# Token products with the weights' low parts last, and another order of normed rows at two stage boundaries, in a hybrid decoder layer

## Chip, cores and metric

The kernel runs on 1 core of one Trainium2 chip. The metric is the time of one execution in microseconds of the device. Engines are named as in the profile: PE is TensorE (matrix products), PEld its weight loads, ACT is ScalarE, DVE is VectorE, POOL is GpSimd, SP is SyncE, which issues the loads.

## The reference

One layer on a sequence of 256 tokens with 1024 channels, all in float32, conditioned by a vector `c`:

```python
c_act = silu(c);  mod = c_act @ w_ada + b_ada;  sh1, sc1, g1, sh2, sc2, g2, sh3, sc3, g3 = split(mod, 9)
u = modulate(rmsnorm(h, norm_ff1), sh1, sc1)
h = h + 0.5 * g1 * swiglu(u, w_ff1_gate, w_ff1_up, w_ff1_down)      # 2816 hidden columns
u = modulate(rmsnorm(h, norm_mix), sh2, sc2)
h = h + g2 * token_mixing(u, ...)     # proj = u @ w_in; gated linear attention and block attention, 4 heads each
u = modulate(rmsnorm(h, norm_ff2), sh3, sc3)
h = h + 0.5 * g3 * swiglu(u, w_ff2_gate, w_ff2_up, w_ff2_down)
return rmsnorm(h, norm_final)
```

`rmsnorm(x, g)` is `x * rsqrt(mean(x*x) + 1e-6) * g`, `modulate(x, sh, sc)` is `x * (1 + sc) + sh`, and `swiglu` is `(silu(x @ w_gate) * (x @ w_up)) @ w_down`.

## The kernel before

Activations lie with channels on the 128 partitions: 8 blocks of channels by 256 tokens. Each product of full precision is made of three products of rounded parts: with `x = xh + xl` and `w = wh + wl`, it is `wh*xh + wh*xl + wl*xh`, and all three are added up in one accumulation bank (`mm3`). A weight tile of 128 by about 1024 is loaded by SP (`load`, 8 buffers called `raw`); ACT rounds it to its high part (`hi`), DVE takes the difference to get the low part (`lo`); both have 6 buffers (`split`). `Stream` holds the tiles in the order of their use: `more` or `prepare` does load, `hi` and `lo` of the next tile, `high` does load and `hi` and returns a function that issues the `lo` later, `take` hands out the oldest prepared tile, and `ahead(n)` prepares until n are ready. Instructions of PE, ACT and DVE stay in the order in which the program issues them (`InOrder`), so an instruction that waits holds all those behind it on its engine.

Between two parts of the layer stands a `Boundary`. It ends the last accumulations (`finish`), adds them to `h` block by block and makes rounded rows of `h` without the norm. `first` runs the first 24 blocks of products (8 channel blocks by 3 weight tiles, `mm3` each) with these unnormed rows, so that PE works while the mean square is made. On the way, at block 14, PE sums the squares and POOL takes the power -0.5 (line 388); later `spread` (line 426) brings 1/rms to all partitions by two transposes on PE. Then `modulate` makes the normed rows by a written-out order: step `n` k (DVE) multiplies row block k by the gain and 1/rms, `h` k (ACT) adds the shift and rounds it to the high part, `l` k (DVE) makes the low part. In the same order `A` prepares a whole weight tile, `H` loads one and makes its high part, `L` makes the low part of the oldest tile that `H` began, `b` (ACT) copies 1/rms out of its bank (`rbs`), and `s` loads a table for ACT. `MOD1` is the order of the first boundary, `MOD2` that of the second. The block order is `IN_TURN` = 0 4 1 5 2 6 3 7 for accumulations; `MOD1` goes by 0 to 7.

Behind the first boundary the next products are those of `gv_t`, a `Tokens` (line 780): here the rows are the stationary operand and the weight tile is the moving one, 4 weight tiles of 2 channel blocks each, 2 halves of the tokens (`t`), 2 halves of 264 columns: 96 products. The inner loop takes, for one bank at a time,

```python
mm(to, b, u2[0][:, k, blk(t)], wh[:, ws])
mm(to, b, u2[1][:, k, blk(t)], wh[:, ws])
mm(to, b, u2[0][:, k, blk(t)], wl[:, ws], stop=(k == KD - 1))
```

Then the three banks of `first` are multiplied by `rbs` (`normed`: `col` on ACT, `sg` on DVE, `gqk` on ACT), the banks of `gv_t` are copied (`glt`, then `v`), and the order `MIX` runs the mixing: jobs of column products (`F`, 48 or 24 products) between the steps of the two attentions. Its first words are `F lowrank F logits`: the logits need `glr`, which ACT copies behind the tiles that the first `F` prepares. A second `Tokens`, `mv_t`, has one piece of 512 columns.

Behind the second boundary `START2` (line 58) gives the order: `t` runs two gate products together (`both_gates`: at each channel block the two banks take turns), `i` scales the three banks of `first`, `A` prepares a tile, `o` runs `low_last` (16 products with the high part of a tile, then 8 with the low part), `s` and `m` make the first hidden rows, `r` splits them in parts, and `g` goes on with a third row. Then come a gate-and-up job of 48 products and the first down job, for which five tiles are prepared.

Of the kernel before, what the change touches and what calls it, by code (L numbers as in the profile page):

```python
# [20 lines left out]
KD = D // P  # L21
# [31 lines left out]
         q7 l4 a6 a7 l5"""  # L53
LAST = """n0 q0 n1 q1 a0 s0 n2 q2 a1 s1 n3 q3 a2 s2 n4 q4 a3 s3 n5 q5 a4 s4 n6 q6 a5 s5 n7 q7 z7 s6 a6 a7"""
LATE = "l6 l7"
MOD1 = "A H n0 h0 n1 h1 l0 n2 h2 l1 n3 h3 l2 l3 L n4 h4 n5 h5 l4 n6 l5 A h6 n7 h7 l6 l7 A b"
MOD2 = "A H s n0 h0 n4 h4 n1 l0 h1 l4 n5 h5 l1 n2 h2 l5 n6 h6 l2 n3 h3 l6 n7 h7 l3 l7 L A b"
START2 = "t i0 i1 i2 A o s0 s2 m0 g m1 g r0 r1 g"
GV = 528
EPS = 1e-6  # L60
NEG = -1e30
# [28 lines left out]
def hybrid_layer(ctx: ExitStack, tc: tile.TileContext, x, xT, cols, tri_d, mask_d, rel_bias,  # L90
# [16 lines left out]
    class InOrder:  # L107


        def __init__(self, engine):  # L110
            self.engine, self.last, self.on = engine, None, False
# [19 lines left out]
    def name(s):  # L131
        n_made[0] += 1
        return f"{s}_{n_made[0]}"

    def bank():
        return pp.tile([P, 512], F32, tag="b", name=name("b"), bufs=8)
# [4 lines left out]
    def big():  # L141
        return wk.tile([P, KD, S], F32, tag="b8", name=name("b8"), bufs=2)
# [6 lines left out]
    def mid(shape, dt=F32):  # L149
        return wk.tile(shape, dt, tag="s4", name=name("s4"), bufs=MID)  # L150

    def row(shape=(P, S), dt=F32, tag="r1", bufs=6):
        return wk.tile(list(shape), dt, tag=tag, name=name(tag), bufs=bufs)

    def blk(i):
        return slice(i * P, (i + 1) * P)

    def wblk(i):
        return slice(i * P + i // 4 * 32, (i + 1) * P + i // 4 * 32)

    def play(order, ops):

        for word in order.split():
            op = word.rstrip("0123456789")
            ops[op](*[int(x) for x in word[len(op):]])
# [42 lines left out]
    def mm(out_ap, bank_t, lhsT, rhs, stop=False):  # L208

        first = id(bank_t) not in opened  # L210
        i = ten.matmul(out_ap, lhsT, rhs, start=first, stop=stop, skip_group_check=True)
        last_mm[0] = i
        if first:
            opened[id(bank_t)] = (i, bank_t)
        else:
            tc.add_manual_dep(i.ins, opened[id(bank_t)][0].ins.name, DEP, reason="the bank's first matmul")
        return i

    def mm3(out_ap, bank_t, w, wsl, a, stop=False):

        wh, wl = w
        ah, al = a
        mm(out_ap, bank_t, wh[:, wsl], ah)
        mm(out_ap, bank_t, wh[:, wsl], al)
        mm(out_ap, bank_t, wl[:, wsl], ah, stop=stop)
# [36 lines left out]
    stream = Stream()  # L262

    class Pipe:
# [10 lines left out]
        def run(self, job):  # L275
            due = job()
            self.fetch()
            self.due = due
            stream.ahead(self.depth)

        def next(self):
            if self.todo:
                self.run(self.todo.pop(0))
# [182 lines left out]
    def low_last(b, base, w, u):  # L466

        for part in range(2):
            for k in IN_TURN:
                for r in range(2 - part):  # L470
                    mm(b[:, base:base + S], b, w[part][:, wblk(k)], u[r][:, k, :S], stop=(k == KD - 1 and part == 1))
# [42 lines left out]
    class Boundary:  # L514
# [46 lines left out]
        def first(self, parts, late, sum_at=14):  # L561


            blocks = [(k, b, w) for k in IN_TURN for b, w in parts]
            for at, (k, b, w) in enumerate(blocks):
                if at == sum_at:
                    self.rms.sums()
                    self.steps(late)
                if at == sum_at + 2 * len(parts):
                    self.rms.spread()  # L570
                mm3(b[:, :SW], b, w, wblk(k), (self.uh[:, k, :SW], self.ul[:, k, :SW]), stop=(k == KD - 1))

# [36 lines left out]
    ada_raw, lead_raw, ws, us = {}, {}, {}, {}  # L609
# [39 lines left out]
    rests = {}  # L649
# [24 lines left out]
    for f in range(LEAD, NF):  # L674
        stream.unit(("gu1", f), gu1[f - LEAD])
        work1.append(("f", f))
        n = sum(1 for x, _ in work1 if x == "d")
# [22 lines left out]
    for f in range(NF):  # L700
        stream.unit(("gu2", f), gu2[f])
        work2.append(("f", f))
        n = sum(1 for x, _ in work2 if x == "d")
# [33 lines left out]
    hid = Hidden()  # L737
    steps = [hid.add(b) for b in lead_banks]
# [13 lines left out]
    def mix_constants():  # L752
        ctri = [load(tri_d[:, i]) for i in range(3)]
        for to, src in ((mask, mask_d), (rel, rel_bias), (wlr_s, wlr)):
            nc.sync.dma_start(to, src)
        for i in range(3):
            act.activation(tri[:, i], ctri[i][:, :512], AF.Copy)
        bank()

        nc.gpsimd.memset(rrow, NEG)  # L760
        for bucket, first, last in BUCKETS:
            nc.gpsimd.tensor_copy(rrow[:, 127 + first:128 + last],
                                  rel[:, bucket:bucket + 1].to_broadcast([4, last - first + 1]))
        nc.gpsimd.dma_start(rdram, rrow)
        nc.gpsimd.dma_start(bias, bass.AP(tensor=rdram.tensor, offset=rdram[:, :].offset,
                                          ap=[[1, P], [NREL, 4], [1, S]]))
        vec.memset(glr, 1.0)
# [12 lines left out]
    class Tokens:  # L780


        def __init__(self, *widths):
            self.width, self.pieces = sum(widths), []
            for n in widths:
                at = self.pieces[-1].stop if self.pieces else 0
                self.pieces.append(slice(at, at + n))

        def run(self, i):
            if i == 0:  # L790
                self.banks = [[bank() for _ in self.pieces] for _ in range(2)]
            wh, wl = stream.take()
            for kk in range(2):
                k = 2 * i + kk
                for t in range(2):
                    for b, piece in zip(self.banks[t], self.pieces):
                        ws = slice(kk * self.width + piece.start, kk * self.width + piece.stop)
                        to = b[:, :piece.stop - piece.start]
                        mm(to, b, u2[0][:, k, blk(t)], wh[:, ws])
                        mm(to, b, u2[1][:, k, blk(t)], wh[:, ws])  # L800
                        mm(to, b, u2[0][:, k, blk(t)], wl[:, ws], stop=(k == KD - 1))

    def columns(done):

# [17 lines left out]
    pipe.depth = AHEAD2  # L822
    h = bd.new
    fb = [bank() for _ in range(3)]
    gv_t = Tokens(GV // 2, GV // 2)
    bd.first([(b, stream.take()) for b in fb], LATE)
    u2 = bd.modulate(MOD1)
    gk, gq = [row(tag="gqk", bufs=4) for _ in range(2)], [row(tag="gqk", bufs=4) for _ in range(2)]
    mk, mq = mid([P, 4, S]), mid([P, 4, S])
    mv_t = Tokens(512)  # L830
    got = {}

    def to_sbuf(dst, scale=1.0):
# [36 lines left out]
    for i, (to, scale) in enumerate(((gk[0], 1.0), (gk[1], 1.0), (gq[0], GLA_SCALE))):  # L870
        t, col = bd.normed(fb[i], scale)
# [59 lines left out]
    at = [mid([P, 4, S]), mid([P, 4, P])]  # L931
# [217 lines left out]
    pipe.depth = AHEAD4  # L1149
    hid = Hidden()  # L1150
    sb = [bank(), bank()]
    sg, m, steps = {}, {}, hid.add(sb[1], 2)

    def both_gates():
        together([(b, 0, stream.take()) for b in sb], u3)
# [7 lines left out]
    def first_product(i):  # L1163
# [3 lines left out]
        else:  # L1167
            vec.tensor_tensor(out=m[1], in0=sg[2], in1=sb[0][:, :S], op=ALU.mult)

    play(START2, {"A": stream.more, "t": both_gates, "i": normed_part, "s": first_silu, "m": first_product,  # L1170
                  "r": lambda i: hid.add_rows(m[i], i), "o": lambda: low_last(sb[1], S, stream.take(), u3),
                  "g": lambda: next(steps)})
    dbanks = []
    for at, (what, n) in enumerate(work2[3:-1]):
        pipe.run(gate_up(hid, u3) if what == "f" else down(n, dbanks, hid))
# [23 lines left out]
    o = big().rearrange("p k s -> p (k s)")  # L1199
    rs = bd.rms.rs  # L1200

    def scaled(engine, t, at, n):

        src, dst = turned_o[t][at // 512][:, at % 512:at % 512 + n], o[:, t * D + at:t * D + at + n]
        if engine is act:
            act.activation(dst, src, AF.Copy, scale=rs[:, t:t + 1])
        else:
            vec.tensor_scalar(dst, src, rs[:, t:t + 1], None, op0=ALU.mult)
        return out[blk(t), at:at + n], dst

    pieces = [scaled(vec, 0, 512, 256), scaled(act, 0, 0, 512), scaled(vec, 0, 768, 256), scaled(vec, 1, 512, 512)]
# [102 lines left out]
```

## Time and profile before

| | us |
|---|---|
| median of 3 runs | 571.19 |
| lowest and highest run | 570.15, 572.04 |
| the profiled execution | 570.41 |
| its span in the trace | 568.6 |

The profile is that of one execution. Its span runs from the first to the last recorded instruction; the time of the execution is 1.8 us longer. In lists of instructions each row has the start in us from the span's start, the length, the engine, line 115 (where a helper records every operation), the operation, output and inputs by the program's names, their form, and a count where several in a row are merged. A bracket at the end names how long the engine stood before and what ended that. Rows of PE overlap, since products are pipelined: their starts tell the pace.

### The profile page before, as it was taken

What the parts mean: (1) busy time and instruction counts of PE and PEld (TensorE: products, weight loads), DVE (VectorE), ACT (ScalarE), POOL (GpSimd) and SP (SyncE); (2) the same over time, 40 slices, a digit from 0 to 9 for tenths busy, and PEclk for the clock granted to TensorE, in tenths of its full rate; (3) what the DMA queues carried; (4) which work ended last, traced back from release to release, by engine and by line L of the source; (5) the groups of instructions that cost most, each with busy time, mean ns of one, the idle gap of its engine ahead of it and who ended that gap; (6) DMA issues with size and microseconds to landing.
All of it is one profiled execution on the core that took longest, in us unless ns stands there. A gap on an engine that the chain in (4) does not pass through costs nothing.

```text
span 568.6 us, 11729 instructions
## 1 busy us (share of the span) xinstructions
PE 556.6 (98%) x4740; PEld 549.9 (97%) x4740; DVE 443.2 (78%) x685; ACT 302.5 (53%) x483; POOL 17.4 (3%) x49
## 2 busy tenths in 40 slices
PE   7999999999999999999999999999999999999995
PEld 7999999999999998998999999999999999999995
DVE  6999887788897887899998979789884656655534
ACT  5557753345445747843864543585644454454424
POOL 1000050000000100000001000000000000000000
PEclk9999999999999999999999999999999999999998
DMA  8999789999998536554399778833897566775102
GB/s 312 406 408 408 251 276 382 407 361 362 329 369 296 182 101 198 184 176 158 117 303 379 278 269 266 298 129 106 270 358 226 190 206 222 243 250 184 46 1 75
DMA packets 39567, 141.92 MB, mean 250 GB/s; under 512 B 4549, under 2 KB 4954, under 8 KB 39386
## 3 DMA queue, kind: packets, MB, share of 16 engines
q1 hardware_dynamic: 39194, 140.39, 70.6%
q8 instruction: 37, 0.61, 0.4%
q0 software_dynamic: 176, 0.53, 0.3%
q10 hardware_dynamic: 144, 0.26, 0.1%
q14 instruction: 16, 0.13, 0.1%
HBM read 140.11 MB, written 1.05 MB: 248 GB/s over the span
## 4 chain that ended last, share of the span: by engine, by line
PE 55%; issue 32%; DVE 6%; DMA 3%; ACT 2%; SPq 0%; POOLq 0%; POOL 0%; DVEq 0%; ACTq 0%
PE b L115 55%; DVE lo L115 2%; DMA raw<-in_lead 2%; DVE b L115 1%; ACT hi L115 1%; DMA raw<-in_adal 1%; DVE s L115 1%; DVE raw L115 1%; ACT ub L115 1%; DVE n L115 0%; DVE ub L115 0%; ACT gqk L115 0%; DVE sg L115 0%; ACT s L115 0%; SPq L292 0%
## 5 line engine op out<-in xcount | busy, mean ns | idle before, releaser
L115 PE MATMUL b<-ub,hi 128*128 128x256 f32 (+1 forms) x1920 | 329.1, 278 | 0.8 <-ACT ub L115 0.3
L115 PEld LDWEIGHTS b<-ub,hi 128*128 128x128 f32 x1920 | 287.3, 188 | 2.1 <-ACT ub L115 0.5
L115 DVE TENSOR_TENSOR lo<-raw,hi 128x1024 fp32r<-128x1024 f32 (+2 forms) x189 | 225.3, 1218 | 65.8 <-ACT hi L115 64.2
L115 PE MATMUL b<-ub,lo 128*128 128x256 f32 (+1 forms) x960 | 259.6, 277 | 0.0
L115 ACT ACTIVATE hi<-raw 128x1024 fp32r<-128x1024 f32 (+2 forms) x189 | 193.2, 1049 | 73.0 <-issue 31.5
L115 PEld LDWEIGHTS b<-ub,lo 128*128 128x128 f32 x960 | 177.7, 188 | 0.0
L115 PE MATMUL b<-s,hi 128*128 128x256 f32 x960 | 164.7, 276 | 0.0
L115 PEld LDWEIGHTS b<-s,hi 128*128 128x128 f32 x960 | 144.4, 188 | 0.0
L115 PE MATMUL b<-s,lo 128*128 128x256 f32 x480 | 132.6, 276 | 0.3 <-DVE lo L115 0.3
L115 PEld LDWEIGHTS b<-s,lo 128*128 128x128 f32 x480 | 90.1, 188 | 0.5 <-DVE lo L115 0.5
L115 DVE SCALAR_TENSOR_TENSOR raw<-raw,cact 128x1024 f32<-128x1024 f32 (+1 forms) x64 | 75.8, 1220 | 0.5 <-DMA raw<-in_adal 0.5
L115 ACT ACTIVATE s<-m 128x256 fp32r<-128x256 f32 x52 | 21.4, 417 | 79.3 <-DVE m L115 79.3
L115 ACT ACTIVATE sg<-b 128x256 f32<-128x256 f32 x46 | 17.1, 380 | 46.2 <-PE b L115 44.3
L115 DVE TENSOR_TENSOR s<-m,s 128x256 fp32r<-128x256 f32 x52 | 21.8, 424 | 20.7 <-ACT s L115 20.5
L115 DVE TENSOR_TENSOR m<-sg,b 128x256 f32<-128x256 f32 x43 | 17.8, 417 | 13.2 <-ACT sg L115 13.1
L115 ACT ACTIVATE s<-b 128x256 f32<-128x256 f32 (+4 forms) x34 | 14.1, 462 | 23.8 <-PE b L115 21.0
L115 PE MATMUL b<-hi,ub 128*128 128x264 f32 (+1 forms) x96 | 22.2, 322 | 0.1
L115 PEld LDWEIGHTS b<-hi,ub 128*128 128x128 f32 x96 | 15.8, 188 | 1.5 <-DVE ub L115 0.3
L388 POOL TENSOR_TENSOR tiny<-tiny,mhalf 128x2 f32<-128x2 f32 (+1 forms) x5 | 5.6, 1113 | 366.4 <-DVE tiny L115 366.4
L115 PE MATMUL b<-lo,ub 128*128 128x264 f32 (+1 forms) x48 | 15.7, 328 | 0.7 <-DVE lo L115 0.6
L115 DVE SCALAR_TENSOR_TENSOR b<-b,mods,b 128x256 f32<-128x256 f32 x24 | 10.6, 480 | 4.5 <-PE b L115 4.5
L115 ACT ACTIVATE ub<-n,mods 128x256 fp32r<-128x256 f32 x16 | 7.8, 507 | 11.1 <-DVE n L115 11.1
(127 smaller groups left out, 285.7 us busy)
## 6 DMA issues: line engine op xcount, KB each, us to landing
raw<-in_gu SPq DMA_DIRECT2D x72, 512.0 KB, 5.8
raw<-in_ada SPq DMA_DIRECT2D x56, 512.0 KB, 5.9
raw<-in_dn SPq DMA_DIRECT2D x44, 512.0 KB, 5.9
raw<-in_win SPq DMA_DIRECT2D x24, 512.0 KB, 4.3
raw<-in_adal SPq DMA_DIRECT2D x16, 513.0 KB, 8.3
raw<-in_lead SPq DMA_DIRECT2D x16, 512.0 KB, 7.9
raw<-in_gbr SPq DMA_DIRECT2D x16, 512.0 KB, 6.7
raw<-in_wout SPq DMA_DIRECT2D x8, 512.0 KB, 6.3
```

What stands on the lines that cost most here:

```text
L115: x = getattr(self.engine, op)(*args, **kw)
L388: nc.gpsimd.tensor_tensor(out=rs[:, :n], in0=ms[:, :n], in1=mhalf[:, :n], op=ALU.pow)
```

## The change

Four edits. `Tokens` takes a width and a number of pieces, and changes the order of its products: for each tile all products with the high part first, those with the low part last; for the first tile, the four products with the high part of a row before the four with its low part. `MOD1` goes two normed rows ahead of ACT and puts the low parts of three weight tiles, each begun by `H`, between the rows. `spread` comes one block of products sooner, at both boundaries. `START2` begins one more weight tile by `H` and makes its low part between the two first hidden rows.

```diff
-MOD1 = "A H n0 h0 n1 h1 l0 n2 h2 l1 n3 h3 l2 l3 L n4 h4 n5 h5 l4 n6 l5 A h6 n7 h7 l6 l7 A b"
+MOD1 = "A H n0 h0 n1 h1 n2 l0 h2 l1 n3 h3 l2 n4 h4 l3 n5 h5 L H l4 n6 h6 l5 n7 h7 l6 L H l7 L b"
-START2 = "t i0 i1 i2 A o s0 s2 m0 g m1 g r0 r1 g"
+START2 = "t i0 i1 i2 A o H s0 s2 m0 g L m1 g r0 r1 g"
...
-                if at == sum_at + 2 * len(parts):
+                if at == sum_at + 2 * len(parts) - 1:
                     self.rms.spread()
...
-        def __init__(self, *widths):
-            self.width, self.pieces = sum(widths), []
-            for n in widths:
-                at = self.pieces[-1].stop if self.pieces else 0
-                self.pieces.append(slice(at, at + n))
+        def __init__(self, width, pieces):
+            self.width, self.pieces, self.cols = width, pieces, width // pieces
...
-            for kk in range(2):
+
+            first = [(kk, r, 0) for kk in range(2) for r in range(2)] if i == 0 else [(kk, None, 0) for kk in range(2)]
+            for kk, r, low in first + [(0, 0, 1), (1, 0, 1)]:
                 k = 2 * i + kk
                 for t in range(2):
-                    for b, piece in zip(self.banks[t], self.pieces):
-                        ws = slice(kk * self.width + piece.start, kk * self.width + piece.stop)
-                        to = b[:, :piece.stop - piece.start]
-                        mm(to, b, u2[0][:, k, blk(t)], wh[:, ws])
-                        mm(to, b, u2[1][:, k, blk(t)], wh[:, ws])
-                        mm(to, b, u2[0][:, k, blk(t)], wl[:, ws], stop=(k == KD - 1))
+                    for c, b in enumerate(self.banks[t]):
+                        ws = slice(kk * self.width + c * self.cols, kk * self.width + (c + 1) * self.cols)
+                        for rr in ((0, 1) if r is None else (r,)):
+                            mm(b[:, :self.cols], b, u2[rr][:, k, blk(t)], (wl if low else wh)[:, ws],
+                               stop=(low == 1 and k == KD - 1))
...
-    gv_t = Tokens(GV // 2, GV // 2)
+    gv_t = Tokens(GV, 2)
...
-    mv_t = Tokens(512)
+    mv_t = Tokens(512, 1)
...
-    sg, m, steps = {}, {}, hid.add(sb[1], 2)
+    sg, m, rests, steps = {}, {}, [], hid.add(sb[1], 2)
...
-                  "g": lambda: next(steps)})
+                  "g": lambda: next(steps), "H": lambda: rests.append(stream.high()), "L": lambda: rests.pop(0)()})
```

## Rows read from the trace of the kernel before

**Rows 1.** The page's table of engines: busy us, share of the span, instructions.
```profile
PE 556.6 (98%) x4740; PEld 549.9 (97%) x4740; DVE 443.2 (78%) x685; ACT 302.5 (53%) x483; POOL 17.4 (3%) x49
```

**Rows 2.** PE in order of time, from the spread to the logits.
```profile
201.63 0.38 PE L115 MATMUL b<-ident,tiny 128*128 128x128 f32 x2
...
203.30 0.75 PE L115 MATMUL b<-hi,ub 128*128 128x264 f32 x2
...
204.01 0.41 PE L115 MATMUL b<-hi,ub 128*128 128x264 f32 x2
...
206.56 0.40 PE L115 MATMUL b<-hi,ub 128*128 128x264 f32 x2
207.14 0.39 PE L115 MATMUL b<-lo,ub 128*128 128x264 f32 x1 [0.18 <-DVE lo L115]
...
210.75 0.39 PE L115 MATMUL b<-lo,ub 128*128 128x264 f32 x1 [0.43 <-DVE lo L115]
...
214.01 0.39 PE L115 MATMUL b<-lo,ub 128*128 128x264 f32 x1
...
216.81 0.39 PE L115 MATMUL b<-ub,hi 128*128 128x256 f32 x2
...
222.39 0.28 PE L115 MATMUL b<-ub,lo 128*128 128x256 f32 x1
223.62 1.13 PE L115 MATMUL b<-wlr_s,glr 17*128 17x256 f32 x4 [0.95 <-ACT glr L115]
```

**Rows 3.** DVE in order of time at the first boundary.
```profile
200.44 1.25 DVE L115 TENSOR_TENSOR lo<-raw,hi 128x1056 fp32r<-128x1056 f32 x1
202.05 0.87 DVE L115 SCALAR_TENSOR_TENSOR n<-b,mods,b 128x256 f32<-128x256 f32 x2 [0.36 <-PE b L115]
...
209.44 1.26 DVE L115 TENSOR_TENSOR lo<-raw,hi 128x1056 fp32r<-128x1056 f32 x1
...
212.70 3.58 DVE L115 TENSOR_TENSOR lo<-raw,hi 128x1056 fp32r<-128x1056 f32 x3 [0.49 <-ACT hi L115]
216.19 0.42 DVE L115 TENSOR_TENSOR sg<-b,rbs 128x256 f32<-128x256 f32 x1
```

**Rows 4.** ACT in order of time, first boundary to the logits.
```profile
202.57 0.96 ACT L115 ACTIVATE ub<-n,mods 128x256 fp32r<-128x256 f32 x2 [3.08 <-DVE n L115]
...
220.36 2.99 ACT L115 ACTIVATE hi<-raw 128x1024 fp32r<-128x1024 f32 x3
223.21 0.36 ACT L115 ACTIVATE glr<-b 16x256 f32<-16x256 f32 x1
```

**Rows 5.** PE in order of time behind the second boundary.
```profile
386.83 0.40 PE L115 MATMUL b<-ub,hi 128*128 128x256 f32 x2
...
395.45 0.39 PE L115 MATMUL b<-ub,hi 128*128 128x256 f32 x2
...
401.23 0.39 PE L115 MATMUL b<-s,hi 128*128 128x256 f32 x2
401.91 0.39 PE L115 MATMUL b<-s,lo 128*128 128x256 f32 x1 [0.30 <-DVE lo L115]
```

**Rows 6.** DVE in order of time behind the second boundary.
```profile
385.58 1.26 DVE L115 SCALAR_TENSOR_TENSOR n<-b,mods,b 128x256 f32<-128x256 f32 x3 [0.40 <-PE b L115]
...
399.50 5.76 DVE L115 TENSOR_TENSOR lo<-raw,hi 128x1024 fp32r<-128x1024 f32 x5 [0.44 <-ACT hi L115]
```

**Rows 7.** POOL in order of time at the two boundaries.
```profile
199.88 0.83 POOL L388 TENSOR_TENSOR tiny<-tiny,mhalf 128x2 f32<-128x2 f32 x1 [3.20 <-DVE tiny L115]
...
383.42 0.78 POOL L388 TENSOR_TENSOR tiny<-tiny,mhalf 128x2 f32<-128x2 f32 x1 [76.19 <-DVE tiny L115]
```

**Rows 8.** Windows: stretch, its length, busy of PE, PEld, DVE, ACT, POOL, granted clock, DMA.
```profile
267.00:300.00 33.00, 33.00 (x274) 32.48 (x274) 32.27 (x72) 22.95 (x48) 0.00 (x0) 1.00 0.60 200
386.83:395.45 8.62, 8.62 (x75) 8.55 (x74) 8.36 (x19) 6.02 (x14) 0.00 (x0) 1.00 0.24 72
```

**Rows 9.** ACT in order of time behind the second boundary.
```profile
394.96 0.51 ACT L115 ACTIVATE sg<-sg,col 128x256 f32<-128x256 f32 x1 [0.81 <-DVE sg L115]
```

More of the change, by code (lines that the diff above doesn't have):

```diff
@@ L780, in hybrid_layer @@
     class Tokens:
-        def __init__(self, *widths):
-            self.width, self.pieces = sum(widths), []
-            for n in widths:
-                at = self.pieces[-1].stop if self.pieces else 0
-                self.pieces.append(slice(at, at + n))
+        def __init__(self, width, pieces):
+            self.width, self.pieces, self.cols = width, pieces, width // pieces
         def run(self, i):
             if i == 0:
-                self.banks = [[bank() for _ in self.pieces] for _ in range(2)]
+                self.banks = [[bank() for _ in range(self.pieces)] for _ in range(2)]
             wh, wl = stream.take()
-            for kk in range(2):
+            first = [(kk, r, 0) for kk in range(2) for r in range(2)] if i == 0 else [(kk, None, 0) for kk in range(2)]
+            for kk, r, low in first + [(0, 0, 1), (1, 0, 1)]:
                 k = 2 * i + kk
                 for t in range(2):
-                    for b, piece in zip(self.banks[t], self.pieces):
-                        ws = slice(kk * self.width + piece.start, kk * self.width + piece.stop)
-                        to = b[:, :piece.stop - piece.start]
-                        mm(to, b, u2[0][:, k, blk(t)], wh[:, ws])
-                        mm(to, b, u2[1][:, k, blk(t)], wh[:, ws])
-                        mm(to, b, u2[0][:, k, blk(t)], wl[:, ws], stop=(k == KD - 1))
+                    for c, b in enumerate(self.banks[t]):
[3 more added lines that the diff above has]
+                               stop=(low == 1 and k == KD - 1))
     def columns(done):
```

## The prediction

> **What bounds the kernel now.** I read the page's table of engines first [rows 1]: TensorE (PE) is busy 98% of the span, so only the few microseconds in which it waits, or runs below its steady pace, can be won. Then I read PE in order of time through the two stretches that the diff touches.
>
> The first stretch is the one behind the first boundary. The 24 blocks of `first` end at 203.30, the 96 products of `gv_t` run until 216.81, and the products of the rest start there [rows 2]. The undisturbed pace is seen between 204.01 and 206.56: seven groups of three products in 2.55 us, 0.364 a group, 0.1213 a product. 96 products at that pace are 11.65 us; the stretch takes 13.51. So **1.86 us** are lost in it. The rows say where. The first group lasts 0.71 instead of 0.36: its second product waits for the low part of the normed row. Then, three times, the two products with the high part of a weight tile are done and the third stands until VectorE has made the low part: at 207.14 and 210.75 the row names `lo` itself, at 214.01 none is named, but there too the third product stands on a row of its own, apart from its pair.
>
> VectorE (DVE) shows why [rows 3]: the low part of the third tile starts at 209.44, that of the fourth is the first of three at 212.70, because in MOD1 both stand far back, behind normed rows that themselves wait for ScalarE (ACT).
>
> Behind the products a second wait: PE has finished its second column job at 222.39 + 0.11 = 222.50 and starts the logits at 223.62 [rows 2], 1.12 us later, on `glr`. ACT makes `glr` behind three `hi` tiles [rows 4], and those stand behind a chain that begins with DVE's first `sg` at 216.19 [rows 3]. From that `sg` to the logits are 7.43 us.
>
> The second stretch is behind the second boundary. Between 395.45 and 401.23 PE does 51 products in 5.78 us, 0.1133 each [rows 5]. At this pace the 72 products of `both_gates` and `low_last` from 386.83 on are 8.16 us; they take 8.62, so **0.46 us** are lost. And the product at 401.91 could have started at 401.23 + 0.23 = 401.46; it waited **0.45 us** for `lo` [rows 5], the second of five tiles that DVE splits from 399.50 on [rows 6]: 399.50 + 1.13 + 1.25 = 401.88.
>
> In all 1.86 + 1.12 + 0.46 + 0.45 = 3.89 us of loss lie where the diff can reach them.
>
> **Spread one block sooner.** In both boundaries the two transposes move ahead of three products, 0.36 us by the group above. They need 1/rms: POOL ends at 199.88 + 0.83 = 200.71, and the transposes would start at 201.63 - 0.36 = 201.27; in the second boundary POOL ends at 384.20 and DVE's first row waits for PE until 385.58 [rows 2, 3, 6, 7]. So the transposes don't wait, and PE does the same work. DVE's first `n` starts 0.36 sooner, at 201.69; DVE would be free, since its `lo` from 200.44 ends at 201.69 [rows 3]. If POOL were late PE itself would stand, but 0.56 us of slack say no. I take 0.36 in both places; the bounds are 0 and 0.36.
>
> **MOD1.** Nothing is added or removed: one tile is still prepared whole at the start and three more are taken, in the same order, with the same eight `n`, `h` and `l`; loads come off SP in the same order. Only the order on DVE and ACT is new: n0 n1 n2 l0 l1 n3 l2 n4 l3 n5 L l4 n6 l5 n7 l6 L l7 L on DVE. Steps of `n` and `l` start 0.39 apart (0.87 for two, 0.48 for one), those of `lo` 1.165 apart (3.58 for three, 1.25 for one) [rows 3]. ACT needs 0.51 for an `h`, and the next one starts 0.45 behind it (0.96 for two) [rows 4]. With two rows ahead DVE never waits: h0 can end at 201.69 + 0.48 + 0.04 + 0.51 = 202.72, and l0's turn comes at 201.69 + 3 x 0.39 = 202.86, so l0 is there at 203.34. All other pairs lie at least that far apart. I therefore add up DVE's own steps. First L (tile 2): behind ten steps, 201.69 + 3.93 = 205.62, done at 206.87. Second L (tile 3): 201.69 + 15 x 0.393 + 1.165 = 208.75, done at 210.0. l7 starts at 209.9. Third L (tile 4): 210.31, done at 211.56. On ACT the `hi` of tile 3 stands behind h5 and is done near 207.2, that of tile 4 behind h7, near 209.9 (1.07 each, [rows 4] have three in 2.99).
>
> **Token products.** The number stays 96, each with its own weight load, and so does the width of 264. New is when PE asks for what, counted from 203.30 at 0.1213. l0: after 4 products, 203.79, ready at 203.34. Low part of tile 2: after 24 + 16 = 40, at 208.15, ready at 206.87. `hi` of tile 3: after 48, at 209.12, ready near 207.2; its low part: after 64, at 211.06, ready at 210.0. `hi` of tile 4: after 72, at 212.03, ready near 209.9; its low part: after 88, at 213.97, ready at 211.56. The smallest slack is 0.45 us, the next 1.05. So no wait is left, and the products end at 203.30 + 11.65 = 214.95: **1.86 us sooner**. If the slack at l0 fails, the loss is a few tenths; the lower bound is the old 1.86 lost again.
>
> Could the new order itself cost? Now most products write another accumulation bank than the one before. The nearest row is `both_gates`, which changes the bank at every product: granted clock 1.00 over 386.83 to 395.45 [rows 8], and I found its loss to be waits for rows. So I take nothing; the other end is a rival below. `mv_t` gets the same order; its PE rows show no wait today, so I take 0.
>
> **What follows it.** DVE's steps behind the third L are the low parts of the next two tiles and then the first `sg`: 210.31 + 3 x 1.165 = 213.81, instead of 216.19: 2.38 sooner. The chain of 7.43 us from there is ACT and DVE work that keeps its order, and PE is no part of it except for the end of the products (214.95, long before ACT copies the banks behind its three `gqk` steps). So the logits can start at 213.81 + 7.43 = 221.24; PE arrives at 222.50 - 1.86 = 220.64 and waits 0.60 instead of 1.12. **2.38 us** are won by then. It must also pass 220 to 300, where DVE is busy 32.27 of 33 us from 267 on [rows 8] and PE 33.00: both are at their limit. The win passes if both arrive sooner by the same amount, which is so here: DVE, ACT and PE all are 2.38 early at the logits, and the tiles that they then need were loaded up to eight ahead. I take all of it; bounds 1.2 and 2.9 (the glr wait gone too).
>
> **Second boundary.** With 1/rms 0.36 sooner, n, h and l come 0.36 sooner. Today PE falls behind them by 0.46 over `both_gates`, in steps of about a tenth; early rows give this back but for a tenth at most. I take **0.46**; bounds 0.3 and 0.46. START2 takes one unit more, the first tile of the down job: its `hi` on ACT behind the `hi` of A, where ACT today stands 0.81 us before `sg` at 394.96 [rows 9], its `lo` on DVE between m0 and m1. What is queued behind it, m1, the gated product and the hidden rows, comes 1.17 later less 0.36. Today the low parts of those rows end before the five tiles start at 399.50, so they would end before 400.31 at the latest; the down job starts behind 48 products, at 395.45 - 0.46 + 5.44 = 400.43. They are hidden, the last of them narrowly. The second tile of that job is then the first of four: today the first tile's `hi` is done at 399.46 (its `lo` at 399.50 waited for it [rows 6]); now the second tile's `hi` stands in that place, later by some 0.55 of the 0.81, since part of it is a wait already. Done near 400.0, its `lo` 1.25 later, at 401.25; PE asks at 401.46 - 0.46 = 401.0. So 0.45 becomes about 0.27. I take **0.18**; bounds -0.3 (hidden rows late) and 0.45.
>
> **Sum.** 2.38 + 0.46 + 0.18 = 3.02. The profiled execution takes 570.41 (span 568.6 and 1.8 around it), so 567.4; the median of the runs is 0.78 above the profiled one, so **568.2** on that scale.
>
> **Rivals.** *VectorE keeps its waits.* If DVE, in the new order, still stands for ACT between the rows, its `sg` moves little, and what PE wins at the products it spends in front of `glr` or of DVE's next results. For it: DVE's 32.27 of 33 us later on [rows 8], where nothing could be caught up. Against it: two rows of distance are worth 0.8 us of DVE, an `h` takes 0.51. Win 1.2 + 0.6 = 1.8: 569.4.
>
> *Given back later.* Some fixed thing, a transfer or an engine that I took to move along, holds the mixing stage, and all is waited for again. For it: the small margins between PE and DVE. Against it: no PE wait in the trace names a DMA. 571.0.
>
> *Bank changes slow PE, and the kernel is slower.* The place is the stage of the 96 products: if a change of bank at most products left gaps and the granted clock fell from 2.4 to 1.2 GHz there, the products would take up to twice 11.65 us; less the 3.0, some 9 us more: 580. Against it stands the granted clock of 1.00 where banks change at every product [rows 8]. It decides against the change from 26% of such a slowing on (3.0 of 11.65).
>
> The Trainium skill speaks for this rival: "TensorE: Matmul & The Clock Gate", section "A second HAM failure mode: psum-queue depth-cycling", tells of a kernel that cycled through banks and in which PE idled so often between groups that its clock gate went back and forth. By that rule the time would be the 580 of the rival. The trace doesn't agree: the stretch with a bank change at every product ran at a granted clock of 1.00 [rows 8].
>
> *The spread waits for POOL.* Then the change does not do what it says there: 0.36 less in each boundary, and PE stands. The 0.56 of slack make it unlikely; it would give 569.0, inside the range.
>
> **Chances.** Forecast, with the small variants that end within 567.2 to 569.2: 0.65. VectorE keeps its waits, near 569.4: 0.18. Given back, near 571.0: 0.13. Slower: 0.04. The runs of before lie between 570.15 and 572.04, so 0.3% (1.7 us) is about what can be told from no change; 569.5 is the border of faster. All of the forecast and some two thirds of the second case lie below it: faster 0.77. The rest of the second case and the third: same 0.19. Slower 0.04. The range holds the forecast and most of the second case, 0.8 in all, with the bounds of its terms and the spread of medians: 566.9 to 569.9.
>
> **What will show it.** Right: the 96 products take about 11.7 us with no gap before a low part; DVE runs from n0 to the first `sg` without a wait, 12.1 us; the first `n` starts 0.36 sooner behind its POOL step; the wait for `glr` is near 0.6; `both_gates` and `low_last` take 8.2; the wait for `lo` in the first down job is about 0.3. Wrong: gaps in DVE between `n` and `l`; a longer wait for `glr`, or a new one for DVE near 265; the hidden rows late at the first down job; a granted clock below 1.00 in the products.

## The result, and the profile after

The changed kernel takes 567.15 us (median of 6 runs, 566.94 to 567.29), the kernel before it 570.83 beside it (570.15 to 572.04). The ratio is 0.9933, interval 0.9919 to 0.9946: **0.7% faster**, 3.7 us. The profiled execution takes 566.94, its span is 565.1.

PE of the changed kernel in order of time, from the spread to the logits, answers to [rows 2]:

```profile
200.77 0.38 PE L115 MATMUL b<-ident,tiny 128*128 128x128 f32 x2
...
202.79 2.12 PE L115 MATMUL b<-hi,ub 128*128 128x264 f32 x16
204.75 1.13 PE L115 MATMUL b<-lo,ub 128*128 128x264 f32 x8
205.72 2.12 PE L115 MATMUL b<-hi,ub 128*128 128x264 f32 x16
207.68 1.14 PE L115 MATMUL b<-lo,ub 128*128 128x264 f32 x8
208.66 2.10 PE L115 MATMUL b<-hi,ub 128*128 128x264 f32 x16
210.60 1.13 PE L115 MATMUL b<-lo,ub 128*128 128x264 f32 x8
211.56 2.11 PE L115 MATMUL b<-hi,ub 128*128 128x264 f32 x16
213.51 1.14 PE L115 MATMUL b<-lo,ub 128*128 128x264 f32 x8
214.48 0.40 PE L115 MATMUL b<-ub,hi 128*128 128x256 f32 x2
...
220.08 0.28 PE L115 MATMUL b<-ub,lo 128*128 128x256 f32 x1
220.70 1.13 PE L115 MATMUL b<-wlr_s,glr 17*128 17x256 f32 x4 [0.34 <-ACT glr L115]
```

Four times sixteen products with the high part of a tile and eight with the low part, and no row names a wait: 214.48 - 202.79 = 11.69 us for the 96, where [rows 2] had 13.51. The last product before the logits starts at 220.08 and is through 0.11 later; the logits start at 220.70, so the wait for `glr` is 0.51 us where it was 1.12.

DVE over the same stretch, for [rows 3]:

```profile
199.93 1.25 DVE L115 TENSOR_TENSOR lo<-raw,hi 128x1056 fp32r<-128x1056 f32 x1
201.19 1.26 DVE L115 SCALAR_TENSOR_TENSOR n<-b,mods,b 128x256 f32<-128x256 f32 x3
202.37 0.87 DVE L115 SCALAR_TENSOR_TENSOR ub<-n,mods,ub 128x256 fp32r<-128x256 f32 x2
...
205.13 1.25 DVE L115 TENSOR_TENSOR lo<-raw,hi 128x1056 fp32r<-128x1056 f32 x1
...
208.27 1.25 DVE L115 TENSOR_TENSOR lo<-raw,hi 128x1056 fp32r<-128x1056 f32 x1
209.44 0.48 DVE L115 SCALAR_TENSOR_TENSOR ub<-n,mods,ub 128x256 fp32r<-128x256 f32 x1
209.84 3.52 DVE L115 TENSOR_TENSOR lo<-raw,hi 128x1056 fp32r<-128x1056 f32 x3
213.28 0.42 DVE L115 TENSOR_TENSOR sg<-b,rbs 128x256 f32<-128x256 f32 x1
```

Not one bracket stands between the first `n` and the first `sg`: 12.09 us without a wait, where [rows 3] had 14.14 with several. And the first `n` follows its `lo` at once; it no longer waits for PE. POOL is through with 1/rms at 199.38 + 0.83 = 200.21, 0.56 us before the transposes at 200.77 (for [rows 7]):

```profile
199.38 0.83 POOL L388 TENSOR_TENSOR tiny<-tiny,mhalf 128x2 f32<-128x2 f32 x1 [3.19 <-DVE tiny L115]
```

ACT comes to `glr` by the same chain as before, sooner (for [rows 4]):

```profile
217.44 2.99 ACT L115 ACTIVATE hi<-raw 128x1024 fp32r<-128x1024 f32 x3
220.29 0.35 ACT L115 ACTIVATE glr<-b 16x256 f32<-16x256 f32 x1
```

Behind the second boundary, PE and then DVE (for [rows 5] and [rows 6]):

```profile
383.94 0.40 PE L115 MATMUL b<-ub,hi 128*128 128x256 f32 x2
...
392.21 0.39 PE L115 MATMUL b<-ub,hi 128*128 128x256 f32 x2
...
397.99 0.39 PE L115 MATMUL b<-s,hi 128*128 128x256 f32 x2
398.38 0.39 PE L115 MATMUL b<-s,lo 128*128 128x256 f32 x1
```

```profile
382.33 1.26 DVE L115 SCALAR_TENSOR_TENSOR n<-b,mods,b 128x256 f32<-128x256 f32 x3
...
393.79 1.22 DVE L115 TENSOR_TENSOR lo<-raw,hi 128x1024 fp32r<-128x1024 f32 x1
...
397.10 4.63 DVE L115 TENSOR_TENSOR lo<-raw,hi 128x1024 fp32r<-128x1024 f32 x4 [0.43 <-ACT hi L115]
```

The 72 products of `both_gates` and `low_last` take 8.27 instead of 8.62. The tile that START2 begins early has its `lo` at 393.79; the next tile is now the first of four, and the third product of its first block, due at 397.99 + 0.23, starts at 398.38: 0.16 us late instead of 0.45.

### The profile page after: what moved, and what is told of

The parts are those of the page before. It is cut to its first block, busy times and chain, and to the rows that moved or that the text cites. A ratio compares the mean times of both kernels' runs of the same rounds, so it can differ in the third digit from the quotient of the medians.

```text
span 565.1 us, 11728 instructions
## 1 busy us (share of the span) xinstructions
PE 554.5 (98%) x4740; PEld 548.5 (97%) x4740; DVE 442.8 (78%) x685; ACT 303.2 (54%) x483; POOL 17.4 (3%) x49
## 3 DMA queue, kind: packets, MB, share of 16 engines
HBM read 140.11 MB, written 1.05 MB: 250 GB/s over the span
## 4 chain that ended last, share of the span: by engine, by line
PE 55%; issue 32%; DVE 7%; DMA 3%; ACT 2%; SPq 0%; POOLq 0%; POOL 0%; DVEq 0%; ACTq 0%
PE b L115 55%; DVE lo L115 3%; DMA raw<-in_lead 2%; DVE b L115 1%; DMA raw<-in_adal 1%; DVE s L115 1%; ACT hi L115 1%; DVE raw L115 1%; DVE ub L115 1%; DVE n L115 1%; ACT gqk L115 0%; DVE sg L115 0%; ACT ub L115 0%; ACT s L115 0%; SPq L292 0%
## 5 line engine op out<-in xcount | busy, mean ns | idle before, releaser
L115 PE MATMUL b<-hi,ub 128*128 128x264 f32 (+1 forms) x96 | 16.6, 321 | 0.0
L115 PEld LDWEIGHTS b<-hi,ub 128*128 128x128 f32 x96 | 13.9, 188 | 1.2
L115 ACT ACTIVATE sq<-b 128x256 f32<-128x256 f32 x24 | 9.2, 408 | 5.6 <-DVE b L115 5.0
```

Of the source, the lines that this page charges most:

```text
L115: x = getattr(self.engine, op)(*args, **kw)
```

## The experiments

The table is read from each run's trace: differences between starts of PE's rows. "Products" are the 96 token products, "to the logits" counts from the first of them, "on to boundary 2" from the logits to the first product of `both_gates`, "gates" are its 72 products, "down" the wait in the first down job. Times are medians; the runs come from three groups, each on one chip: the first with the four rows below the whole change, the second with the next four, the third with the last four. The kernel before took 570.39, 571.08 and 570.25 us beside them.

| run | products | to the logits | on to boundary 2 | gates | down | time, us |
|---|---|---|---|---|---|---|
| before | 13.51 | 20.32 | 163.21 | 8.62 | 0.45 | 570.83 |
| whole change | 11.69 | 17.91 | 163.24 | 8.27 | 0.16 | 567.15 |
| tokens alone | 12.45 | 20.31 | 163.26 | 8.64 | 0.43 | 570.53 |
| MOD1 alone | 12.84 | 18.62 | 163.22 | 8.62 | 0.44 | 568.73 |
| all but tokens | 12.49 | 18.27 | 163.19 | 8.27 | 0.17 | 567.68 |
| spread alone | 13.13 | 19.96 | 164.83 | 8.38 | 0.32 | 569.81 |
| all but START2 | 11.68 | 17.90 | 163.23 | 8.28 | 0.44 | 567.41 |
| glr sooner | 11.68 | 17.48 | 163.45 | 8.27 | 0.17 | 567.15 |
| glr sooner, old tokens | 12.50 | 18.27 | 163.19 | 8.26 | 0.18 | 567.76 |
| bank every product | 11.68 | 17.90 | 163.24 | 8.29 | 0.16 | 567.13 |
| whole change again | 11.69 | 17.90 | 163.22 | 8.27 | 0.17 | 567.16 |
| glr later | 11.69 | 18.84 | 164.89 | 8.28 | 0.15 | 568.98 |
| three tiles until D0 | 11.69 | 17.49 | 163.29 | 8.27 | 0.17 | 566.90 |
| glr sooner again | 11.68 | 17.49 | 163.43 | 8.27 | 0.16 | 566.96 |

**The new token order alone.** The edit, against the changed kernel:

```diff
-MOD1 = "A H n0 h0 n1 h1 n2 l0 h2 l1 n3 h3 l2 n4 h4 l3 n5 h5 L H l4 n6 h6 l5 n7 h7 l6 L H l7 L b"
-START2 = "t i0 i1 i2 A o H s0 s2 m0 g L m1 g r0 r1 g"
+MOD1 = "A H n0 h0 n1 h1 l0 n2 h2 l1 n3 h3 l2 l3 L n4 h4 n5 h5 l4 n6 l5 A h6 n7 h7 l6 l7 A b"
+START2 = "t i0 i1 i2 A o s0 s2 m0 g m1 g r0 r1 g"
...
-                if at == sum_at + 2 * len(parts) - 1:
+                if at == sum_at + 2 * len(parts):
```

Expected: 

> Only the new order of the token products; MOD1, spread and START2 as in the kernel before. Theory A (the chain of VectorE and ScalarE that ends in glr sets when the logits start): PE saves some 1.2 us in the 96 products, but the first sg stays where it was, so the logits start no sooner and the wait for glr grows from 1.1 to about 2.3 us; time as before, 0.0 +- 0.2 us. Rival B (the waits of PE in the products are what the change wins): 1.2 us or more faster.

Measured: 570.53 us, ratio 0.9997 (0.9984 to 1.001). PE wins 1.06 us in the products and has none of it at the logits, 20.31 after the first product as before. Its rows show where it went:

```profile
214.46 1.14 PE L115 MATMUL b<-lo,ub 128*128 128x264 f32 x8
...
219.08 0.39 PE L115 MATMUL b<-ident,glt 128*16 128x128 f32 x2 [0.74 <-ACT glt L115]
...
223.30 1.13 PE L115 MATMUL b<-wlr_s,glr 17*128 17x256 f32 x4 [1.00 <-ACT glr L115]
```

The wait for `glr` did not grow to the 2.3 us that I expected; a second wait, for `glt` in front of the first transposes, took its part. By starts the two are 0.90 and 1.16 us, 2.06 together, and both end with ACT. Theory A holds, rival B falls.

**MOD1 alone.**

```diff
-                if at == sum_at + 2 * len(parts) - 1:
+                if at == sum_at + 2 * len(parts):
...
-            for kk, r, low in first + [(0, 0, 1), (1, 0, 1)]:
...
+            for kk in range(2):
...
+                        for rr, part in ((0, wh), (1, wh), (0, wl)):
+                            mm(b[:, :self.cols], b, u2[rr][:, k, blk(t)], part[:, ws],
+                               stop=(part is wl and k == KD - 1))
...
-START2 = "t i0 i1 i2 A o H s0 s2 m0 g L m1 g r0 r1 g"
+START2 = "t i0 i1 i2 A o s0 s2 m0 g m1 g r0 r1 g"
```

Expected: 

> Only the new order of MOD1; token products, spread and START2 as before. Theory A: VectorE runs without a gap, its first sg comes 2.0 us sooner and with it glr and the logits, 2.0 us faster, while PE still waits some 1.0 us between the products (a low row and the low parts of tiles 2 and 3). Rival B: the products' waits go only in part, 0.9 us faster.

Measured: 568.73 us, ratio 0.9958 (0.9942 to 0.9974). The logits come 1.70 us sooner: nearer to A's 2.0 than to B's 0.9. The products take 12.84, so they still lose 1.2 us, and now PE, with no wait for `glr` left, is the later of the two: that is what is missing to 2.0. So this one line of order is worth more than half of the whole change.

**All but the token order.**

```diff
-            for kk, r, low in first + [(0, 0, 1), (1, 0, 1)]:
...
+            for kk in range(2):
...
+                        for rr, part in ((0, wh), (1, wh), (0, wl)):
+                            mm(b[:, :self.cols], b, u2[rr][:, k, blk(t)], part[:, ws],
+                               stop=(part is wl and k == KD - 1))
```

Expected: 

> All of the change except the new order of the token products. Theory A: PE waits some 0.6 us in the products (low parts of tiles 2 and 3), this comes out of its wait for glr, which shrinks to nearly nothing; the time is that of the whole change, +- 0.2 us. Rival B: slower than the whole change by the waits that come back, 0.6 us or more.

Measured: 567.68 us, ratio 0.9942 (0.9926 to 0.9958). Neither was right. The products lose 12.49 - 11.65 = 0.84 us, not 0.6, so PE again has no wait for `glr` and comes 0.36 us later to the logits than with the whole change. At the logits the token order is worth 0.36 on top of the rest, less than its 0.80 in the products, because the wait for `glr` takes up the difference. The times lie 0.53 apart; the traces, from the first token product to the end of the span, 0.30.

**The spread alone.**

```diff
-MOD1 = "A H n0 h0 n1 h1 n2 l0 h2 l1 n3 h3 l2 n4 h4 l3 n5 h5 L H l4 n6 h6 l5 n7 h7 l6 L H l7 L b"
+MOD1 = "A H n0 h0 n1 h1 l0 n2 h2 l1 n3 h3 l2 l3 L n4 h4 n5 h5 l4 n6 l5 A h6 n7 h7 l6 l7 A b"
...
+                        for rr, part in ((0, wh), (1, wh), (0, wl)):
...
-START2 = "t i0 i1 i2 A o H s0 s2 m0 g L m1 g r0 r1 g"
+START2 = "t i0 i1 i2 A o s0 s2 m0 g m1 g r0 r1 g"
```

Expected: 

> Only the spread one block sooner. If the rows of both boundaries simply come 0.36 us sooner: 0.36 us at the logits and about 0.35 us over the two gates behind the second boundary, 0.7 us faster in all, with PE's waits at the token products still there. Rival C (the earlier transposes only make PE stand, or the rows are held by something else): 0.0.

Measured: 569.81 us, ratio 0.9977 (0.9965 to 0.999), which is 0.6 under the 570.39 beside it; rival C falls. The logits come 0.36 sooner, the number of the prediction, and behind the second boundary the gates take 0.24 less and the wait in the down job is 0.13 shorter. But from the logits to the second boundary its profile takes 1.6 us longer than any run above it. The windows of this profile (stretch, length, busy of PE, PEld, DVE, ACT, POOL, granted clock, DMA) show where:

```profile
222.00:224.00 2.00, 1.02 (x6) 0.67 (x5) 2.00 (x3) 2.00 (x4) 0.00 (x0) 1.00 0.29 82
224.00:226.00 2.00, 2.00 (x11) 1.77 (x10) 2.00 (x3) 1.98 (x3) 0.00 (x0) 0.62 0.92 274
226.00:228.00 2.00, 2.00 (x12) 2.00 (x12) 0.96 (x3) 1.92 (x4) 0.00 (x0) 0.53 0.91 340
228.00:230.00 2.00, 2.00 (x20) 2.00 (x19) 1.56 (x2) 1.97 (x3) 0.00 (x0) 1.00 0.82 322
```

PE waits for `glr` in the first of them, busy 1.02 of 2 us; right behind it the granted clock is near one half, and a window of 2 us holds 11 or 12 products instead of 20. The prediction has nothing of this; the last group of runs was made for it.

**All but START2.**

```diff
-START2 = "t i0 i1 i2 A o H s0 s2 m0 g L m1 g r0 r1 g"
+START2 = "t i0 i1 i2 A o s0 s2 m0 g m1 g r0 r1 g"
```

Expected: 

> All of the change except START2, which is that of before. If the tile begun early is what shortens the wait in the first down job: that wait is 0.45 to 0.55 us instead of 0.16, so 0.3 us slower than the whole change, with nothing else moved. Rival: the wait is shortened by the earlier 1/rms alone, no difference.

Measured: 567.41 us, ratio 0.9932 (0.9919 to 0.9944). The wait in the down job is 0.44 and nothing else differs from the whole change: START2 is worth 0.28 us, all there.

**glr sooner**, with the new and with the old order of the token products (the second has the token edit of "all but the token order" besides):

```diff
-MIX = """F lowrank F logits
+MIX = """F lowrank deep F logits
...
+    def deeper():
+        pipe.depth = AHEAD2
...
+    pipe.depth = AHEAD2 - 1
     play(MIX, ops)
```

Expected: 

> The whole change, and the first column job prepares two weight tiles instead of three before glr is copied (the third follows behind glr). PE's wait for glr, 0.5 us in the whole change, goes. Theory A: PE then runs into the next products that need the logits' low parts, where some 0.2 to 0.3 us come back, so 0.2 to 0.5 us faster than the whole change. Rival: all is given back at the next wait, no difference.

Expected: 

> As the run with glr sooner, but with the old order of the token products. Theory A (the token order is worth something only when glr does not set the logits): the products end some 0.6 us later and the logits with them, so 0.2 to 0.6 us slower than with the new order, about the time of the whole change. Rival: no difference, the token order is worth nothing here either.

Measured: 567.15 us (0.9926, 0.9913 to 0.9939) with the new order, 567.76 (0.9939, 0.9924 to 0.9953) with the old. By the times the first is no faster than the whole change (567.15 in the result, which was not run beside it); its gain stands in the trace alone. The wait for `glr` is gone and the logits come 0.43 sooner than in the whole change; 0.21 of it is lost again before the second boundary. The place is the first decays, `tri`, here first in the whole change and then in this run:

```profile
230.87 1.17 PE L115 MATMUL b<-tri,s 128*128 128x512 f32 x4
```

```profile
230.66 1.41 PE L115 MATMUL b<-tri,s 128*128 128x512 f32 x4
```

The four products take 0.24 longer. The profile names no wait there; DVE has the logits' low part ready at 230.36 + 0.68 = 231.04, and the second of the four starts at 231.10:

```profile
230.36 0.68 DVE L115 TENSOR_TENSOR s<-wide,s 128x512 fp32r<-128x512 f32 x1
```

In the whole change it is ready at 230.72 and that product starts at 231.19. Between the two token orders lie now 0.79 us at the logits: with `glr` out of the way the token order is worth there nearly all that it wins in the products (0.82), as theory A has it. At the second boundary 0.53 of it is left, and 0.61 by the times, the upper end of what was expected.

**A bank change at every product.**

```diff
-            first = [(kk, r, 0) for kk in range(2) for r in range(2)] if i == 0 else [(kk, None, 0) for kk in range(2)]
+            first = [(kk, r, 0) for kk in range(2) for r in range(2)]
```

Expected: 

> The whole change, with the rows' high and low parts apart for all four tiles, so that each of the 96 token products writes another bank than the one before (also the products of the second set with one piece). If a change of bank costs nothing: 11.7 us for the 96 products, clock 1.00, the same time. Rival (changes of bank leave gaps, or the clock falls): the 96 products take longer than 12 us and the kernel is slower by that much, less the 0.5 us of the wait for glr.

Measured: 567.13 us, ratio 0.9927 (0.9914 to 0.9939). The window over its 96 products:

```profile
203.32:215.00 11.68, 11.68 (x98) 11.68 (x97) 11.05 (x20) 7.57 (x14) 0.00 (x0) 1.00 0.53 168
```

11.68 us, granted clock 1.00. The rival that was to make the kernel slower is refuted: taking turns among four banks costs nothing here. This is firmer ground than the window of [rows 8], whose last 24 products, those of `low_last`, all write one bank. The Trainium skill ("TensorE: Matmul & The Clock Gate", "A second HAM failure mode: psum-queue depth-cycling") tells of a kernel that cycled through banks and whose PE idled between groups of products. No run here shows that idling: PE is busy for all of the 11.68 us, so what is shown is that the change of banks alone costs nothing.

**The whole change again, and glr later.** The first is the changed kernel itself; the second makes `glr` wait for four tiles:

```diff
+    pipe.depth = AHEAD2 + 1
     play(MIX, ops)
```

with `deep` and `deeper` as above.

Expected: 

> The whole change, unchanged, beside the next runs: some 567.1 us with little spread, since its longest wait of PE behind the token products is 0.5 us. The kernel before beside it: two groups of times, near 570.3 and near 572.0 us.

Expected: 

> The whole change, but the first column job prepares four weight tiles before glr is copied, so that PE waits some 1.5 us for glr, with no waits in the token products. Theory D (a wait for glr of more than a microsecond is what lets the granted clock fall behind it in some executions, which costs these another 1.7 us): the time falls in two groups, near 568.1 and near 569.8 us, as in the kernel before. Rival E (the second group belongs to the waits in the token products): one group, near 568.1 us.

Measured: 567.16 us (ratio 0.9941, 0.9926 to 0.9955), all six executions between 566.94 and 567.89; and 568.98 (0.9971, 0.9958 to 0.9984) in two groups, six executions from 567.84 to 568.31 and six from 569.66 to 570.44. PE and windows of the second kernel's profile, which fell in the upper group:

```profile
220.62 0.28 PE L115 MATMUL b<-ub,lo 128*128 128x256 f32 x1
222.17 1.12 PE L115 MATMUL b<-wlr_s,glr 17*128 17x256 f32 x4 [1.28 <-ACT glr L115]
223.22 0.51 PE L115 MATMUL b<-ub,hi 128*128 128x256 f32 x2
223.57 0.28 PE L115 MATMUL b<-ub,lo 128*128 128x256 f32 x1
223.69 0.40 PE L115 MATMUL b<-ub,hi 128*128 128x256 f32 x2
...
224.84 0.63 PE L115 MATMUL b<-ub,hi 128*128 128x256 f32 x2
225.27 0.41 PE L115 MATMUL b<-ub,lo 128*128 128x256 f32 x1
225.48 0.63 PE L115 MATMUL b<-ub,hi 128*128 128x256 f32 x2
...
228.38 0.40 PE L115 MATMUL b<-ub,hi 128*128 128x256 f32 x2
```

```profile
220.00:222.00 2.00, 0.89 (x8) 0.69 (x7) 2.00 (x3) 2.00 (x4) 0.00 (x0) 1.00 0.34 59
222.00:224.00 2.00, 1.83 (x10) 1.44 (x11) 1.73 (x2) 1.03 (x4) 0.00 (x0) 1.00 0.94 274
224.00:226.00 2.00, 2.00 (x14) 2.00 (x14) 1.36 (x3) 1.99 (x3) 0.00 (x0) 0.65 0.94 317
226.00:228.00 2.00, 2.00 (x11) 2.00 (x11) 0.88 (x1) 1.98 (x3) 0.00 (x0) 0.50 0.93 350
```

PE waits 222.17 - 220.62 - 0.11 = 1.44 us for `glr`. A group of three products takes 0.64 us from 224.84 on (225.48 - 224.84); at the full clock it takes 0.34 (three at 0.1133). From the logits to the second boundary this execution needs 164.89 instead of 163.22: **1.67 us**, most of the 1.84 between the medians of the two groups. There is no wait in its token products (11.69), so rival E falls; MOD1 alone, which loses 1.2 us in its products and waits for no `glr`, has one group. Theory D stands: the second group comes and goes with the wait for `glr`. Behind that wait come the four products of the logits, 17 rows each (1.05 us); no run separates them from it.

**Three tiles until D0**, and glr sooner once more:

```diff
-MIX = """F lowrank F logits qk F logs F lparts F diag dset D0 M0
+MIX = """F lowrank F logits qk F logs F lparts F diag dset D0 deep M0
...
+    pipe.depth = AHEAD2 - 1
     play(MIX, ops)
```

Expected: 

> As the run with glr sooner, but only three tiles stay prepared until the first decays (D0), so that ScalarE has one weight tile less before its exponentials. If the 0.2 us that were given back there came from ScalarE: the logits 0.4 us sooner than in the whole change and all of it kept, 566.7 us. If the tile that is missing makes PE wait for low parts later: no gain or up to 1 us slower.

Expected: 

> The run with glr sooner once more, beside the whole change on the same chip: 0.2 us faster than that, as its profile showed; the rival is no difference.

Measured: 566.90 us (ratio 0.9933, 0.9918 to 0.9949) and 566.96 (0.9934, 0.9920 to 0.9948), beside 567.16 of the whole change on that chip. The logits come 0.41 sooner, and 163.29 us later stands the second boundary, so nearly all of it is kept, and `tri` takes 1.17 again:

```profile
230.85 1.17 PE L115 MATMUL b<-tri,s 128*128 128x512 f32 x4
```

What was given back did come from the tile in front of ACT's exponentials. By its trace this version is 0.34 us ahead of the whole change at the second boundary; the times differ by 0.26, and those of glr sooner by 0.20, which their intervals do not separate.

## Why the prediction was right

The forecast was 3.02 us by the trace. Counted from the first token product to the end of the span, the profile before has 568.6 - 203.30 = 365.30 us, the one after 565.1 - 202.79 = 362.31: **2.99 us**.

- *Spread.* Right. The first `n` starts where DVE ends its `lo`, with no wait for PE; alone it moves the logits by 0.36. POOL did not hold it: the slack is the 0.56 that was read before.
- *MOD1.* Right: DVE without a wait, 12.09 us against the 12.12 that the steps add up to.
- *Token products.* 1.86 forecast, 1.82 measured, every part in time. The smallest slack was indeed at the first low row.
- *Logits.* 2.38 forecast, 2.41 measured; rest wait 0.60 forecast, 0.51 measured. It was passed on whole: 163.21 us before and 163.24 after from the logits to the second boundary, although DVE and PE are both full there. "VectorE keeps its waits" and "given back later" are refuted.
- *Second boundary.* Mis-sized, both ways: 0.46 forecast for the gates, 0.35 measured; 0.18 for the down job, 0.29 measured. Together 0.64 for 0.64.
- *The scale.* This step failed. I put the median 0.78 above the profiled execution, as before, and so said 568.2; it is 567.15, nearly that of the profiled one. Two things were in it. Half a microsecond is the start: the first token product stands between 202.79 and 203.33 over the fourteen profiles of the table, in front of all that the edits move but the two transposes, and the profile after has the earliest. The profiles differ there in PE's waits for ACT in the first 26 us. The other is the clock. Of 49 executions of the kernel before that were timed beside the experiments, 30 lie between 569.95 and 571.08 and 19 between 571.61 and 572.90; most of the 19 have a mean granted clock of 0.994. The profile before [rows 2] is one of the first kind, the median stood between. The change cut the wait for `glr` from 1.12 to 0.51 us, and none of the 12 timed executions of the whole change, nor of its variants without a long wait, has a second group. So the time came out 1.0 us under the forecast and 0.25 above the lower end of the range. The spread of the kernel before lay open in its three runs (570.15 to 572.04), but the forecast carried it over to the changed kernel as it was.

What the prediction did not see is which edit does what. It gave the products' 1.86 us to the token order and MOD1 together and then took the chain through `sg` as the limit; it did not draw the conclusion that the token order alone must win nothing. The runs show it: 0.01 us at the logits alone, 0.36 on top of the rest, 0.79 when `glr` is out of the way.

## What to carry to other kernels

When an engine waits several times in one stretch, find the chain that ends last behind the stretch: waits taken out of the engine itself are lost again at the next meeting point until that chain moves too (here a change of order on VectorE was worth 1.70 us and the matching order on TensorE nothing without it). In an order written by hand, let the engine that is nearly full run two steps ahead of the one it alternates with and put work that waits for nobody in between (MOD1 does both at once, and no run tells them apart). And a short wait of TensorE can cost more than its length: look at the spread of the times of the kernel, and at the granted clock behind each wait.

## What the runs showed of the hardware that was not expected

Behind a wait of TensorE for `glr` the granted clock fell for some products to half, the lower of the two levels, in a part of the executions. Two profiles show it: the spread alone (wait 1.14 us) and glr later (1.44 us), where it cost 1.6 and 1.67 us, more than the wait. By the times, in two groups, it was 3 of 12 executions with the spread alone, 6 of 12 with glr later, 2 of 12 with the token order alone (wait 1.16 us) and 19 of 49 of the kernel before (1.12 us); for the last two no profile of the upper group was taken. Where that wait is about 0.5 us or less, none of 56 executions showed it; no run has one between 0.5 and 1.1 us. The length of a wait alone does not decide. With three tiles until D0 PE stood idle 1.18 us near the start, longer than the 0.98 us in front of the logits that the profile gives for the spread alone, and the granted clock stayed at 1.00 behind it:

```profile
12.49 1.22 PE L115 MATMUL b<-ub,hi 128*128 128x256 f32 x8 [1.18 <-ACT hi L115]
```

```profile
14.00:16.00 2.00, 2.00 (x20) 2.00 (x19) 2.00 (x3) 1.36 (x3) 0.00 (x0) 1.00 1.03 416
```

What decides whether it falls in a given execution is not shown by these runs.

The Trainium skill ("TensorE: Matmul & The Clock Gate", "What's actually happening") gives the clock as one of two levels, half or full. The trace agrees: 0.64 us for three products that take 0.34 at the full clock, and 0.50 as the lowest granted clock.
